# Storing the first six tiles from a second queue and halving the last tile, in an average pool over windows of 16

## The chip, the cores and the metric

The kernel runs on one core of a Trainium2 chip. The core has several engines that run their own instruction streams beside each other. This kernel uses four: VectorE (DVE in the profile), ScalarE (ACT), GpSimd (POOL) and SyncE (SP). Sixteen DMA engines move data between the large memory (HBM) and the core's own memory, which has 128 partitions. DMAs are issued by an engine's instruction stream, and each issuing engine has a DMA queue of its own. The metric is the device time of one launch in microseconds (us); lower is better.

## The reference

The input is float32, 32 x 256 x 4096. Each run of 16 neighbouring values along the last axis is replaced by its mean, so the output is 32 x 256 x 256.

```
for i in range(output_size):
    start = int(i * length / output_size)
    end = int((i + 1) * length / output_size)
    result[:, :, i] = np.mean(x[:, :, start:end], axis=-1)
```

The input has 134.2 MB and the output 8.4 MB.

## The kernel before, in words

Batch and channels are taken together as 8192 rows of 4096 values. The rows are handled in 16 tiles of 512 rows; a tile puts 4 rows on each of the 128 partitions, which is 64 KB per partition and 8.39 MB in all. The first 15 tiles share one layout: each partition owns 60 consecutive rows (`x_many`, `o_many`, lines 46 and 47), and tile t takes 4 of them. The last tile has its own block of 512 rows (`x_last`, `o_last`).

The loop over tiles starts on line 62. A tile is loaded into one of two buffers of `inpool` by one DMA from SP's queue (line 73). The cells (outputs) of a tile, 1024 per partition, are split in two halves of m = 512:

- for the second half, POOL adds the upper 8 values of each window onto the lower 8, in place (line 76);
- for the first half, DVE sums the 16 values of each window (line 81);
- DVE then sums the 8 values that POOL left in each window of the second half (line 84);
- ACT multiplies all 1024 sums by 1/16, in place (line 87).

The results of the first 15 tiles are collected in `res_many` in the core's memory, those of the last tile in `res_last`. Nothing is stored until the last tile's load has been issued. Then one store of `res_many` (7.86 MB, line 75) is issued behind that load on SP's queue. When the last tile is scaled, two more stores from SP write `res_last` (line 93): 120 partitions, then 8.

A load must wait until the buffer that it fills has been read by DVE (line 84, two tiles earlier), and the stores of SP wait for ACT. The waits are set by the framework. The stores are kept out of its bookkeeping of completions and count up a semaphore `stored` instead, on which SP waits at the end (line 98).

Of the kernel before, what the change touches and what calls it, by code (L numbers as in the profile page):

```python
# [1 line left out]

# [4 lines left out]


@with_exitstack
def kernel(  # L10
    ctx: ExitStack,
    tc: tile.TileContext,
    x: bass.AP,
    output_size: int,
    out: bass.AP,
):

    nc = tc.nc
    F32 = mybir.dt.float32
    X = mybir.AxisListType.X

    batch, channels, length = x.shape
    ob, oc, olen = out.shape
    assert ob == batch and oc == channels and olen == output_size
    assert length % output_size == 0
    window = length // output_size  # L30
    hw = window // 2
    inv_w = 1.0 / float(window)

    P = nc.NUM_PARTITIONS
    R = 4
    rows = batch * channels
    assert rows % (P * R) == 0
    ntiles = rows // (P * R)
    many = (ntiles - 1) * R
    cells = R * output_size  # L40
    m = cells // 2
    cols = R * length

    xr = x.rearrange("b c l -> (b c) l")
    orow = out.rearrange("b c o -> (b c) o")
    x_many = xr[0 : P * many, :].rearrange("(p r) l -> p (r l)", p=P, r=many)
    o_many = orow[0 : P * many, :].rearrange("(p r) o -> p (r o)", p=P, r=many)
    x_last = xr[P * many :, :].rearrange("(p r) l -> p (r l)", p=P, r=R)
    o_last = orow[P * many :, :].rearrange("(p r) o -> p (r o)", p=P, r=R)

    res_many = nc.alloc_sbuf_tensor("res_many", [P, (ntiles - 1) * cells], F32, align_bytes=256)
    res_last = nc.alloc_sbuf_tensor("res_last", [P, cells], F32, align_bytes=256)
    inpool = ctx.enter_context(tc.tile_pool(name="inpool", bufs=2))

    stored = nc.alloc_semaphore("stored")

    def store(out, in_):
        ins = nc.sync.dma_start(out=out, in_=in_)
        tc.no_tile_sem_insts.add(ins.ins.name)
        ins.then_inc(stored, 16)  # L60

    for t in range(ntiles):
        last = t == ntiles - 1
        xbuf = inpool.tile([P, cols + 64], F32, name="xin")
        off = 32 if last else 0
        flat = xbuf[:, off : off + cols]
        xin = flat.rearrange("p (o w) -> p o w", w=window)
        if last:
            res, base, src = res_last, 0, x_last
        else:  # L70
            res, base = res_many, t * cells
            src = x_many[:, t * cols : (t + 1) * cols]
        nc.sync.dma_start(out=flat, in_=src)  # L73
        if last:
            store(o_many, res_many[:, :])
        nc.gpsimd.tensor_add(  # L76
            out=xin[:, m:cells, 0:hw],
            in0=xin[:, m:cells, 0:hw],
            in1=xin[:, m:cells, hw:window],
        )  # L80
        nc.vector.reduce_sum(  # L81
            out=res[:, base : base + m], in_=xin[:, 0:m, :], axis=X
        )
        nc.vector.reduce_sum(  # L84
            out=res[:, base + m : base + cells], in_=xin[:, m:cells, 0:hw], axis=X
        )
        nc.scalar.mul(  # L87
            out=res[:, base : base + cells],
            in_=res[:, base : base + cells],
            mul=inv_w,  # L90
        )
    for lo, hi in ((0, 120), (120, P)):
        store(o_last[lo:hi, :], res_last[lo:hi, :])

    ctx.pop_all().close()
    tc.close()
    tc.compile()  # L97
    nc.sync.wait_ge(stored, 48)
    nc.sync.sem_clear(stored)


# [1 line left out]
_INS = ['x', 'output_size']  # L103
_OUTS = [((32, 256, 256), 'float32')]

_NUMBERS = {'output_size': 256}


# [26 lines left out]
```

## Time and profile before

| | us |
|---|---|
| median of 3 runs (lowest to highest) | 333.39 (333.27 to 333.47) |
| span of the profiled execution (its only time in the profile) | 332.2 |
| DVE busy | 209.7 |
| POOL busy | 139.7 |
| ACT busy | 18.2 |
| one load, from one landing to the next | 19.3 |
| DVE's 16-value sums, one (128x512<-128x8192) | 8.69 |
| DVE's 8-value sums, one (128x512<-128x4096) | 4.42 |
| POOL's addition, one | 8.72 |
| ACT's scaling, one | 1.06 |

The span runs from the first to the last instruction of one execution. Busy times of different engines lie beside each other and do not add up to the span. "SPq" in the profile is SP's queue: the times of its rows are those of issuing a DMA, not of the transfer. Rows with "<-" in brackets name what ended the idle time before an instruction.

### The profile page before, as it was taken

How to read it: one execution, taken by the hardware profiler on the slowest of the kernel's cores; microseconds unless marked ns; L12 is line 12 of the kernel's file. 1: busy time of each engine (PE TensorE's matmuls, PEld its weight loads, DVE VectorE, ACT ScalarE, POOL GpSimd, SP SyncE). 2: the span in 40 equal slices, each digit the busy share in tenths (PEclk: the TensorE clock that was granted, in tenths of full speed). 3: DMA queues.
4: the chain of work that ended last, by engine and by line, in shares of the span. 5: the costliest groups of instructions: out<-in, count | busy, mean ns of one | idle time of the engine just before them, and what ended most of it. 6: DMA issues, size and time to landing. Idle time of an engine off the chain costs nothing.

```text
span 332.2 us, 160 instructions
## 1 busy us (share of the span) xinstructions
DVE 209.7 (63%) x32; ACT 18.2 (5%) x17; POOL 139.7 (42%) x20
## 2 busy tenths in 40 slices
DVE  0029396692939669392956939295683929578392
ACT  1000101000010100001010000101000010101001
POOL 0027090642709064370906337090633709063370
DMA  9898989989898999989898998989899998989897
GB/s 379 379 505 379 505 379 442 442 379 505 379 505 379 481 402 402 481 379 505 379 497 387 466 418 379 505 379 505 379 489 395 418 466 379 505 379 505 363 473 300
DMA packets 2599, 142.61 MB, mean 429 GB/s; under 512 B 295, under 2 KB 295, under 8 KB 423
## 3 DMA queue, kind: packets, MB, share of 16 engines
q1 hardware_dynamic: 2599, 142.61, 99.4%
HBM read 134.22 MB, written 8.39 MB: 429 GB/s over the span
## 4 chain that ended last, share of the span: by engine, by line
DMA 66%; POOL 18%; DVE 11%; POOLq 3%; issue 0%; ACT 0%; SPq 0%
DMA xin<-in_x_dram 66%; POOL xin L76 18%; DVE res_many L84 9%; POOLq L97 3%; DVE res_last L84 1%; ACT res_last L87 0%; SPq L73 0%; POOLq L76 0%
## 5 line engine op out<-in xcount | busy, mean ns | idle before, releaser
L76 POOL TENSOR_TENSOR xin<-xin 128x4096 f32<-128x4096 f32 x16 | 139.5, 8719 | 181.9 <-DMA xin<-in_x_dram 181.9
L81 DVE TENSOR_REDUCE res_many<-xin 128x512 f32<-128x8192 f32 x15 | 130.3, 8686 | 107.3 <-DMA xin<-in_x_dram 107.3
L84 DVE TENSOR_REDUCE res_many<-xin 128x512 f32<-128x4096 f32 x15 | 66.3, 4420 | 2.5 <-POOL xin L76 2.3
L87 ACT ACTIVATE res_many<-res_many 128x1024 f32<-128x1024 f32 x15 | 15.8, 1056 | 289.6 <-DVE res_many L84 289.6
L81 DVE TENSOR_REDUCE res_last<-xin 128x512 f32<-128x8192 f32 x1 | 8.7, 8686 | 6.6 <-DMA xin<-in_x_dram 6.6
L84 DVE TENSOR_REDUCE res_last<-xin 128x512 f32<-128x4096 f32 x1 | 4.4, 4420 | 0.2 <-POOL xin L76 0.2
L87 ACT ACTIVATE res_last<-res_last 128x1024 f32<-128x1024 f32 x1 | 1.1, 1056 | 18.8 <-DVE res_last L84 18.8
L87 ACT ACT_TABLE_LOAD x1 | 1.3, 1283 | 0.7 <-PEq L116 0.7
L116 POOL MEMSET const-float32-0.0<- 128x1 f32 x1 | 0.1, 99 | 0.2 <-issue 0.2
L116 POOL MEMSET const-bfloat16-1.0<- 128x1 bf16 x1 | 0.1, 102 | 0.0
L116 POOL MEMSET const-uint8-127<- 128x1 uint8 x1 | 0.1, 102 | 0.0
L116 POOL MEMSET const-float32-1.0<- 128x1 f32 x1 | 0.1, 99 | 0.0
## 6 DMA issues: line engine op xcount, KB each, us to landing
out_dram<-res_many SPq DMA_DIRECT2D x1, 7680.0 KB
out_dram<-res_last SPq DMA_DIRECT2D x1, 480.0 KB
xin<-in_x_dram SPq DMA_DIRECT2D x16, 25.3
out_dram<-res_last SPq DMA_DIRECT2D x1, 32.0 KB
```

Source lines behind the costliest of these rows:

```text
L76: nc.gpsimd.tensor_add(out=xin[:, m:cells, 0:hw], in0=xin[:, m:cells, 0:hw], in1=xin[:, m:cells, hw:window],)
L81: nc.vector.reduce_sum(out=res[:, base : base + m], in_=xin[:, 0:m, :], axis=X)
L84: nc.vector.reduce_sum(out=res[:, base + m : base + cells], in_=xin[:, m:cells, 0:hw], axis=X)
L87: nc.scalar.mul(out=res[:, base : base + cells], in_=res[:, base : base + cells], mul=inv_w,)
L97: tc.compile()
L116: nc = _bacc.Bacc("TRN2", target_bir_lowering=False, num_devices=1)
```

## The change

Three things are done otherwise:

- The results of the first six tiles (`early` = 16 x 3 // 8 = 6, `cut` = 6144 cells per partition, 24 KB of each partition's 60 KB) are stored by a DMA of their own. It is issued by ACT. In the source it stands in the loop behind tile index 7; in the built program it stands on ACT directly behind the scaling of the sixth tile, and waits for that scaling only.
- The store behind the last load, on SP, writes the other nine tiles (4.72 MB).
- The last tile is loaded by two DMAs, each with half of the columns (32 KB per partition, that is two of the four rows), and each half is summed on its own, with POOL, DVE and ACT instructions of half the size. The two stores of the last tile are unchanged.

SP's wait at the end counts four stores instead of three.

```
-    def store(out, in_):
-        ins = nc.sync.dma_start(out=out, in_=in_)
+    def store(out, in_, engine=nc.sync):
+        ins = engine.dma_start(out=out, in_=in_)
         tc.no_tile_sem_insts.add(ins.ins.name)
         ins.then_inc(stored, 16)
+
+    early = ntiles * 3 // 8
+    cut = early * cells
+
+    def sums(xin, res, base, count):
+        h = count // 2
+        nc.gpsimd.tensor_add(
+            out=xin[:, h:count, 0:hw],
+            in0=xin[:, h:count, 0:hw],
+            in1=xin[:, h:count, hw:window],
+        )
+        nc.vector.reduce_sum(out=res[:, base : base + h], in_=xin[:, 0:h, :], axis=X)
+        nc.vector.reduce_sum(
+            out=res[:, base + h : base + count], in_=xin[:, h:count, 0:hw], axis=X
+        )
+        nc.scalar.mul(
+            out=res[:, base : base + count],
+            in_=res[:, base : base + count],
+            mul=inv_w,
+        )
 
     for t in range(ntiles):
...
-        nc.sync.dma_start(out=flat, in_=src)
         if last:
-            store(o_many, res_many[:, :])
...
+            hc = cols // 2
+            for k in range(2):
+                nc.sync.dma_start(
+                    out=flat[:, k * hc : (k + 1) * hc], in_=src[:, k * hc : (k + 1) * hc]
+                )
+            store(o_many[:, cut:], res_many[:, cut:])
+            for k in range(2):
+                sums(xin[:, k * m : (k + 1) * m, :], res, k * m, m)
+        else:
+            nc.sync.dma_start(out=flat, in_=src)
+            sums(xin, res, base, cells)
+        if t == early + 1:
+            store(o_many[:, 0:cut], res_many[:, 0:cut], nc.scalar)
     for lo, hi in ((0, 120), (120, P)):
         store(o_last[lo:hi, :], res_last[lo:hi, :])
...
-    nc.sync.wait_ge(stored, 48)
+    nc.sync.wait_ge(stored, 64)
```

More of the change, by code (lines that the diff above doesn't have):

```diff
@@ L72 @@
             src = x_many[:, t * cols : (t + 1) * cols]
-        nc.sync.dma_start(out=flat, in_=src)
         if last:
-            store(o_many, res_many[:, :])
[L76 to L91, printed above, removed]
+            hc = cols // 2
[11 more added lines that the diff above has]
+            store(o_many[:, 0:cut], res_many[:, 0:cut], nc.scalar)
     for lo, hi in ((0, 120), (120, P)):
```

## The prediction

> **What bounds the kernel now.** I read the busy table and the DMA lines of the page first, then a table of stages, then the waits of the loading queue, then the order in time of the last 27 us.
>
> The page: busy time per engine, packets of the only DMA queue, and the chain that ended last.
>
> ```profile
> span 332.2 us, 160 instructions
> DVE 209.7 (63%) x32; ACT 18.2 (5%) x17; POOL 139.7 (42%) x20
> q1 hardware_dynamic: 2599, 142.61, 99.4%
> HBM read 134.22 MB, written 8.39 MB: 429 GB/s over the span
> DMA 66%; POOL 18%; DVE 11%; POOLq 3%; issue 0%; ACT 0%; SPq 0%
> ```
>
> The chain gives POOL and DVE 29%, but no engine is above 63%, while the packets of the one queue fill 99.4% of the 16 DMA engines' time. The chain goes through POOL and DVE only because a load must wait for a free buffer. Whether that wait ever leaves the DMA engines without work is seen in the stages: one tile period from the start of the run, two from the middle (columns: stretch and its length, busy time of DVE, ACT, POOL, clock, DMA share, GB/s).
>
> ```profile
> 22.50:41.80 19.30, 13.11 (x2) 1.06 (x1) 8.72 (x1) 1.00 1.00 435
> 119.30:138.60 19.30, 13.07 (x3) 1.06 (x1) 8.72 (x1) 1.00 1.00 435
> 138.60:157.90 19.30, 13.04 (x3) 1.06 (x1) 8.72 (x1) 1.00 1.00 435
> ```
>
> Each tile of 8.39 MB takes 19.3 us at a DMA share of 1.00. The arithmetic of a tile (13.1 us of DVE, 8.7 us of POOL beside it) ends 6 us before the next tile lands. The waits of SP's queue and of the engines say the same from the other side:
>
> ```profile
> SPq L73 <- DVE res_many L84: 185.8, 14, 13.3
> SPq L73 <- DMA xin<-in_x_dram: 94.7, 14, 20.9
> DVE res_many L81 <- DMA xin<-in_x_dram: 107.3, 15, 22.5
> ```
>
> A load is issued 13.3 us after the tile before it landed, that is 19.3 - 13.3 = 6.0 us before the DMA engines have finished the load that is running. So the next packets are always queued. Now the end, in order of time:
>
> ```profile
> 301.95 4.42 DVE L84 TENSOR_REDUCE res_many<-xin 128x512 f32<-128x4096 f32 x1 [0.18 <-POOL xin L76]
> 306.40 1.06 ACT L87 ACTIVATE res_many<-res_many 128x1024 f32<-128x1024 f32 x1 [18.25 <-DVE res_many L84]
> 307.48 0.35 SPq L58 DMA_DIRECT2D out_dram<-res_many  x1
> 312.96 8.69 DVE L81 TENSOR_REDUCE res_last<-xin 128x512 f32<-128x8192 f32 x1 [6.59 <-DMA xin<-in_x_dram]
> 313.07 8.72 POOL L76 TENSOR_TENSOR xin<-xin 128x4096 f32<-128x4096 f32 x1 [11.15 <-DMA xin<-in_x_dram]
> 321.82 4.42 DVE L84 TENSOR_REDUCE res_last<-xin 128x512 f32<-128x4096 f32 x1 [0.17 <-POOL xin L76]
> 326.27 1.06 ACT L87 ACTIVATE res_last<-res_last 128x1024 f32<-128x1024 f32 x1 [18.81 <-DVE res_last L84]
> 327.35 0.74 SPq L58 DMA_DIRECT2D out_dram<-res_last  x2
> ```
>
> The big store (15 tiles, 7.86 MB) is queued at 307.48, 5.5 us before the last load lands at 312.96, and runs behind it. The last tile's arithmetic runs beside that store and hands over its 0.5 MB at 327.35.
>
> The trace's packet records price everything the DMA engines do. A 64 KB load packet lasts 2418 ns, a 60 KB packet of the big store 2267 ns, a 4 KB packet of the last store 159 ns, a completion record 9 ns. A load and a store packet cost the same per byte: (2418 - 2267) ns for 4096 bytes is 36.9 ps per byte, 27.1 GB/s per engine. What is left per packet is 2418 - 65536 x 0.0369 = 2 ns, or by the 4 KB packets 159 - 151 = 8 ns. The engine passes from load to store within some 15 ns. One engine's work is 128 load packets (309.5 us, and 0.7 us more because the 16 first packets last 2.9 to 3.4 us), 8 of the big store (18.1) and 8 or so of the last (1.3): 329.6 us. From the first packet's start, 1.0 us after its issue at 0.73, to the last packet's end it is 330.05 us. So no more than 0.5 us of idle time lies inside, and a change can gain only by raising the rate per engine or lose by lowering it, adding packets, or leaving a hole.
>
> **The change, part by part.** The sum is made against the span of 332.2 us; the profiled execution shows no time besides. The median of the runs is 333.39, so 1.2 us lie around the span, and I leave that 1.2 as it is.
>
> Bytes: 142.61 MB before and after. The first six tiles' 3.15 MB only change places: out of the end, into the middle. Per engine that is 8 packets of 24 KB, 8 x 0.91 = 7.3 us. The end gets 7.3 us shorter and the loads get 7.3 us later; sum 0.
>
> Early store: in the built order it stands on ACT behind the sixth scaling, whose end in the trace is 132.51 + 1.06 = 133.57. Issuing takes 0.35 us by SP's row; ACT then idles 18.3 us for the seventh tile, so 0. Behind it on ACT stand the scalings of tiles 7 to 15, for which nobody waits before the late store at the end: were ACT even held until the store landed, 0. It passes nothing on SP or POOL. In the DMA engines it meets the load of tile 7, and the load of tile 8 queued at 132.5. If packets alternate one to one, 8 pairs of 2.42 + 0.91 us make a mixed stage of 26.6 us. Those loads land later, so DVE starts later, but the next load is still queued at least 6 us ahead (its 13.3 us are unchanged and the loads only take longer). No hole.
>
> Extra packets per engine: 8 of the early store (the late one has 8 of 36 KB in place of 8 of 60 KB) and 8 of the halved last load (16 of 32 KB for 8 of 64 KB), 16 at 2 to 8 ns: 0.03 to 0.13 us. Two more completion records, at 9 ns and a gap of some 6: 0.03 us. On the DMA engines, on the path: +0.06 to +0.16; I take +0.1, in the middle.
>
> Mixing loads and stores: not in the trace, where all packets stand in one queue. Lower end: below nothing, if an engine could carry a store beside a load, at most the 7.3 us of the early store hidden. Upper end: each of the 8 store packets sets the engine back as a cold start does (the first packets' +0.7 us): 5.6 us. The nearest row is the change from load to store within the queue at the end, 15 ns at one passage with full rates on both sides, so I take 0.
>
> The Trainium skill speaks to this point, in "DMA: Bandwidth & Descriptors", section "Issuing engines are not separate DMA queues": DMAs of different issuing engines run on the same 16 DMA engines and interleave, and a second issuer saves issue time alone. By it the sum keeps its +0.1, and the lower end of -7.3 falls away. The same page's table under "Latency and other measured facts" has copies between HBM tensors at 214 GB/s per direction as the full rate; taken as 428 GB/s of both together, against the 435 of the stages above, 1.6% of 26.6 us would be an estimated +0.4 us, and the time 333.9. No row of this case shows two queues.
>
> The end: the late store is 8 packets of 36 KB per engine, 8 x 1.36 = 10.9 us, and cover for the last tile is that much in place of 18.1. The halves: the whole load lands at 312.96 + 7.3 + 0.1 = 320.4, the first half 9.65 us earlier, at 310.7. Tile 15 lands 7.4 later too, at 300.4, its DVE work ends at 313.7, its scaling at 314.9, and the late store is issued then, 5.5 us before the last load lands, as before. DVE does the first half from 313.7: 128x256<-128x4096 has as many elements as the 4.42 us row, and 128x256<-128x2048 costs 2.3 by the line through 8192 and 4096 elements (8686 and 4420 ns), ending at 320.4. Second half: POOL 8.72 / 2 = 4.4 from 320.5 beside DVE's 4.42, then 0.2 wait, 2.3 DVE, 0.6 ACT (half of 1.06 and some): issue of the last stores at 327.9, against 327.35. The late store's packets last until 320.4 + 10.9 = 331.3, so 3.4 us are left (3.7 before: 312.96 + 18.1 - 327.35), and after the 1.0 us from issue to first packet 2.4 us. The halving is what keeps it so: a whole last tile would hand over at 320.4 + 14.4 = 334.8. Cost 0, the late store hides it.
>
> Sum: 332.2 + 0.1 = 332.3 span; 333.39 + 0.1 = 333.5 us.
>
> **The rivals.**
> Rival 1, slower: each passage between the queues costs the engine. Place: the mixed stage, 16 passages per engine. For: it is unseen, and the only disturbed packets of the trace, the cold first ones, lost 0.7 us each. Against: the gapless passage at the end. It decides from 0.67 us (0.2%), or 0.57 beyond the 0.1: 36 ns per passage, 2.1% of the stage. At 100 ns it is 1.6 us, 335.1 us; at the upper bound 339.1.
>
> Rival 2, faster: a store reads the chip's memory while a load writes it, and the engine does both at once. For: opposite directions, and the trace never has both. Against: the per-engine rate is the same 27.1 GB/s for both kinds, which looks like one pipe. Full overlap: 333.5 - 7.3 = 326.2 us; a tenth of it is -0.7, 332.8, and that is the point from which it counts. The late store would still cover the end: only the middle shrinks.
>
> Rival 3, slower: the halved tail does not fit under the late store. If a half costs POOL 8.72, DVE 4.42 and ACT 1.06 as the whole does, the last stores are issued at 320.5 + 8.72 + 0.2 + 4.42 + 1.06 = 334.9, the first packet is at 335.9, 8 packets at 0.155 and the landing make a span of 337.7, 338.9 us. Against: DVE's two shapes scale with their elements to 2%.
>
> **How the numbers follow.** About 0.2% (0.67 us) is what a measurement of this kernel can tell from no change. Forecast, DMA time unchanged but for the packets: 0.57, 333.5 us, own range 332.8 to 334.0. Rival 1: 0.28; rival 3: 0.03; together slower 0.31. Rival 2: faster 0.12. The range is 332.7 to 336.0: it leaves out rival 2 (0.12), and above 336.0, where a passage costs more than 150 ns, 0.08.
>
> **What would show it.** In the profile after: a second queue of 3.15 MB; a sum of both queues' packet shares near 99%; a stage from 134 to 160 at 435 GB/s with a share of 1.00; the last load landing near 320.4; the last stores issued near 327.9 and ending 4.4 us later. A mixed stage below 435 GB/s, with longer packets or holes, is rival 1; above 435 GB/s, rival 2; a gap of DMA between late and last store, rival 3. I am wrong if the rate of the mixed stage differs by more than 2%, or if the DMA engines run dry where loads of tiles 7 to 9 meet the store.

## The result

The changed kernel takes 334.15 us (334.02 to 334.43) against 333.39 us (medians of 12 runs each): a ratio of 1.0022, 95% interval 1.0014 to 1.0029. It is slower by 0.76 us, a little more than the 0.67 us that the prediction called the least that can be told from no change, and the interval lies clear of 1. The 333.5 us forecast was too low by 0.65 us; the range 332.7 to 336.0 holds the time. The side on which it fell, slower, had been given 0.31; the case "unchanged but for the packets", with 0.57 and its own range up to 334.0, was missed by 0.15 us.

The span of the profiled execution grew from 332.2 to 332.8 us. What lies around the span is 1.30 us for the changed kernel and 1.31 us for the kernel before, each over the repeated runs, so the whole loss lies inside the span.

The page of the changed kernel: busy times, the two DMA queues, and the chain that ended last.

```profile
span 332.8 us, 166 instructions
DVE 209.6 (63%) x34; ACT 18.4 (6%) x18; POOL 139.9 (42%) x21
q1 hardware_dynamic: 2743, 139.46, 97.2%
q10 hardware_dynamic: 144, 3.15, 2.2%
HBM read 134.22 MB, written 8.39 MB: 429 GB/s over the span
DMA 62%; POOL 21%; DVE 14%; DVEq 1%; issue 0%; ACT 0%; POOLq 0%
```

The same bytes now stand in two queues, and their packets again fill 99.4% of the DMA engines' time (97.2 and 2.2). The DMA engines are the bound as before; DVE and POOL do the same work in the same time. So each engine must have spent more time on the same bytes.

Stages around the early store show where (columns: stretch and its length, busy time of DVE, ACT, POOL, clock, DMA share, GB/s; a packet is counted where it starts, so the cuts lie between packets).

```profile
130.30:135.20 4.90, 2.22 (x1) 1.06 (x1) 0.00 (x0) 1.00 0.99 428
135.20:140.30 5.10, 0.00 (x0) 0.00 (x0) 0.00 (x0) 1.00 0.99 360
140.30:160.23 19.93, 13.10 (x2) 1.06 (x1) 8.72 (x1) 1.00 1.00 434
160.23:179.50 19.27, 13.10 (x2) 0.20 (x1) 8.72 (x1) 1.00 1.00 435
```

The mixed stage proper, 140.30 to 160.23, in which a 64 KB load packet and a 24 KB store packet take turns on every engine, runs at 434 GB/s with the engines full. In the trace's packet records a pair takes 3.32 us there, six times over, where 2418 + 912 ns are 3.33: a passage between the queues costs nothing. The loss lies in the five microseconds before it, at 360 GB/s. There each of the 16 engines has one load packet, started between 135.26 and 135.82, that lasts 2965 to 3494 ns in place of 2418. (The packets last longer while the DMA share is 0.99: the engines are busy, but slower.) It is the packet just ahead of the engine's first store packet. I call the excess the setback: 0.79 us, mean over the engines.

The same thing was in the trace of before, and I had not seen it. The stages around its big store:

```profile
306.60:309.10 2.50, 0.00 (x0) 0.86 (x1) 0.00 (x0) 1.00 0.97 419
309.10:312.00 2.90, 0.00 (x0) 0.00 (x0) 0.00 (x0) 1.00 1.01 362
312.00:330.10 18.10, 13.11 (x2) 1.06 (x1) 8.72 (x1) 1.00 1.00 434
```

The last load packet of each engine, started between 309.12 and 309.66, lasts 2704 to 3159 ns, a setback of 0.50 us, and after it the store runs at full rate. So the change moved a setback that was there and made it larger. Its own late store has none: the packets ahead of it last 1213 ns, all of them.

The end of the changed kernel, in order of time:

```profile
314.53 1.06 ACT L76 ACTIVATE res_many<-res_many 128x1024 f32<-128x1024 f32 x1 [18.30 <-DVE res_many L73]
315.61 0.35 SPq L58 DMA_DIRECT2D out_dram<-res_many  x1
318.74 2.27 DVE L73 TENSOR_REDUCE res_last<-xin 128x256 f32<-128x2048 f32 x1
320.64 4.46 POOL L67 TENSOR_TENSOR xin<-xin 128x2048 f32<-128x2048 f32 x1 [5.18 <-DMA xin<-in_x_dram]
320.94 4.41 DVE L72 TENSOR_REDUCE res_last<-xin 128x256 f32<-128x4096 f32 x1
325.26 2.27 DVE L73 TENSOR_REDUCE res_last<-xin 128x256 f32<-128x2048 f32 x1
327.57 0.63 ACT L76 ACTIVATE res_last<-res_last 128x512 f32<-128x512 f32 x1 [5.89 <-DVE res_last L73]
328.22 0.76 SPq L58 DMA_DIRECT2D out_dram<-res_last  x2
```

The second half lands at 320.6, the last stores are issued at 328.22, and by the packet records the late store's packets end between 330.65 and 331.10, so it hides the hand-over with 2.4 us to spare.

The span's +0.55 us: 0.29 of setback (0.79 - 0.50) and 0.14 of packets (16 of 1213 ns for 8 of 2418 is 0.064; 912 + 1364 for 2267, eight times, is 0.072). The remaining 0.12 is spread over the first packets and the last small stores, and is no more than single executions differ by: the spans of the changed kernel's twelve runs go from 332.7 to 333.1. The medians differ by 0.76 us, 0.2 more than these two executions.

### The profile page after: what moved, and what is told of

Read it like the earlier page. It is cut to its first block, busy times and chain, and to the rows that moved or that the text cites. A ratio compares the mean times of both kernels' runs of the same rounds, so it can differ in the third digit from the quotient of the medians.

```text
span 332.8 us, 166 instructions
## 1 busy us (share of the span) xinstructions
DVE 209.6 (63%) x34; ACT 18.4 (6%) x18; POOL 139.9 (42%) x21
## 3 DMA queue, kind: packets, MB, share of 16 engines
q1 hardware_dynamic: 2743, 139.46, 97.2%
## 4 chain that ended last, share of the span: by engine, by line
DMA 62%; POOL 21%; DVE 14%; DVEq 1%; issue 0%; ACT 0%; POOLq 0%
DMA xin<-in_x_dram 62%; POOL xin L67 21%; DVE res_many L73 11%; DVE res_last L72 3%; DVEq L112 1%; DVE res_last L73 1%; ACT res_last L76 0%; POOLq L67 0%
## 5 line engine op out<-in xcount | busy, mean ns | idle before, releaser
L67 POOL TENSOR_TENSOR xin<-xin 128x4096 f32<-128x4096 f32 (+1 forms) x17 | 139.7, 8216 | 185.0 <-DMA xin<-in_x_dram 185.0
L72 DVE TENSOR_REDUCE res_last<-xin 128x256 f32<-128x4096 f32 x2 | 8.8, 4408 | 0.0
L73 DVE TENSOR_REDUCE res_last<-xin 128x256 f32<-128x2048 f32 x2 | 4.5, 2274 | 0.0
L76 ACT ACTIVATE res_last<-res_last 128x512 f32<-128x512 f32 x2 | 1.3, 630 | 11.4 <-DVE res_last L73 11.4
```

Source lines behind the costliest of these rows:

```text
L67: nc.gpsimd.tensor_add(out=xin[:, h:count, 0:hw], in0=xin[:, h:count, 0:hw], in1=xin[:, h:count, hw:window],)
L72: nc.vector.reduce_sum(out=res[:, base : base + h], in_=xin[:, 0:h, :], axis=X)
L73: nc.vector.reduce_sum(out=res[:, base + h : base + count], in_=xin[:, h:count, 0:hw], axis=X)
L76: nc.scalar.mul(out=res[:, base : base + count], in_=res[:, base : base + count], mul=inv_w,)
```

## The experiments

Where a kernel is a variant of the changed one, its diff is against that, else against the kernel before. Times and ratios are against the kernel before on the same chip. The diffs show the lines that matter, without those between them; left out are `store`'s argument for the engine, where a variant of the kernel before needs it, and the count in SP's wait at the end, which follows the number of stores. Each setback is the mean over the 16 engines in one profiled execution.

**Halving alone, and the early store without a second queue.** Theory A says that the first store of a launch sets the engines back wherever it stands; the rivals blame the second queue (B) or the halving (C).

```
halves_only (against the changed kernel)
-            store(o_many[:, cut:], res_many[:, cut:])
+            store(o_many, res_many[:, :])
-        if t == early + 1:
-            store(o_many[:, 0:cut], res_many[:, 0:cut], nc.scalar)

early_sp (against the changed kernel)
-            store(o_many[:, 0:cut], res_many[:, 0:cut], nc.scalar)
+            store(o_many[:, 0:cut], res_many[:, 0:cut])
```

> The kernel before with the halved last tile alone; one store of 15 tiles from SP. The halved load has 8 more packets per engine, 1213 ns for 32 KB against half of 2418: +0.06 us. Theory A (the setback belongs to the first store of a launch, wherever and from whichever queue): one packet per engine slowed by 0.5 us about 1.6 us after the store's issue, as before; time 333.4 to 333.5. Rival B (the second queue costs the 0.6 us): the same, 333.45. Rival C (the halving costs a good part of it): 333.8 or more.

> The changed kernel with the early store issued from SP, between two loads, no second queue. Theory A: the first store still sets each engine back by 0.5 to 0.8 us, now near 155 us where its turn in SP's queue comes or 1.6 us after its issue at 133.6; the late store sets back nothing; time 333.8 to 334.2. Rival B (the second queue costs the whole 0.6 us): 333.5 us. In between (0.5 us of setback in one queue, 0.8 in another): 333.8.

The halving alone took 333.52 us against 333.46, ratio 1.0003 (0.9994 to 1.0012). The 0.06 us is what its packets were reckoned at, and the upper end of the interval leaves 0.4 us, so C does not explain the loss of 0.76. The setback was 0.15 us in its profiled execution.

The early store from SP took 334.07 us, ratio 1.0019 (1.0010 to 1.0028). That is a loss of 0.61 us with one queue, against 0.76 with two, and the 0.15 between them is less than either interval is wide. B falls as the cause of the whole loss. Here nothing is mixed: in SP's queue the store stands whole between two loads. The stages around it:

```profile
154.60:157.50 2.90, 0.00 (x0) 0.00 (x0) 0.00 (x0) 1.00 1.02 362
157.50:164.90 7.40, 6.45 (x1) 0.00 (x0) 6.34 (x1) 1.00 1.01 434
```

The last load packet ahead of the store is slow again (0.54 us mean), the store itself runs at 434 GB/s. This execution took 333.87 us, 0.20 less than the kernel's median, so its setback may be a small one; whether a second queue adds something to the setback is not settled by these runs. The store was issued at 133.62 and the slow packet started at 154.7, so what goes with the setback is the store's turn on the engine, not its issue. The late store of this kernel had none.

**The big store from ACT, at the end.**

```
act_end (against the kernel before)
-            store(o_many, res_many[:, :])
+            store(o_many, res_many[:, :], nc.scalar)
```

> The kernel before with its one big store issued from ACT in place of SP, at the same place. Bytes and packets as before. Theory A: one setback of 0.5 to 0.8 us about 1.6 us after the issue near 307.5; time 333.4 to 333.7. Rival B (a second queue costs the extra 0.3 us of setback and 0.1 around the span): 333.7 to 333.9. If an idle queue's start is what costs, there are two setbacks, a second one when the last stores go to SP's queue.

334.56 us, ratio 1.0033 (1.0021 to 1.0046), slower than any theory said, for a reason that none of them had. The setback is 0.54 us, as in SP's queue (0.50), and there is no second one. But look at the end:

```profile
307.73 0.37 ACTq L58 DMA_DIRECT2D out_dram<-res_many  x1
315.63 8.69 DVE L81 TENSOR_REDUCE res_last<-xin 128x512 f32<-128x8192 f32 x1 [9.02 <-DMA xin<-in_x_dram]
328.94 1.06 ACT L87 ACTIVATE res_last<-res_last 128x1024 f32<-128x1024 f32 x1 [21.24 <-DVE res_last L84]
330.02 0.77 SPq L58 DMA_DIRECT2D out_dram<-res_last  x2
```

In its own queue the store no longer waits behind the last load but takes turns with it. The last load lands at 315.63 in place of 312.96, the last stores are issued at 330.02 in place of 327.35, only 0.1 to 1.0 us before the big store's packets end, and the end lies open: the big store no longer covers the last stores. Their packets start 0.9 us after the issue and take 0.6 us per engine longer than at 159 ns each. So a second queue does have a price: not in the passages, but in the landing that it puts off.

**The last tile whole.**

```
whole_last (against the kernel before)
-            store(o_many, res_many[:, :])
+            store(o_many[:, 6 * cells :], res_many[:, 6 * cells :])
+        if t == 7:
+            store(o_many[:, 0 : 6 * cells], res_many[:, 0 : 6 * cells], nc.scalar)
```

> The changed kernel without the halving: early store from ACT, last tile loaded and summed whole. The late store (10.9 us) ends near 331.4 and the last tile's hand-over comes 14.4 us after its landing at 320.5, so at 334.9; then 1.0 us to the first packet, 1.4 us of packets and 0.45 us to the span's end: 337.8 us of span, 339.0 us, and 3.5 us or more of idle DMA engines near the end. If the late store hides it in some way I have not seen: 334.1.

340.14 us, ratio 1.0198 (1.0184 to 1.0212).

```profile
320.88 8.69 DVE L81 TENSOR_REDUCE res_last<-xin 128x512 f32<-128x8192 f32 x1 [6.05 <-DMA xin<-in_x_dram]
334.19 1.06 ACT L87 ACTIVATE res_last<-res_last 128x1024 f32<-128x1024 f32 x1 [18.27 <-DVE res_last L84]
335.27 0.74 SPq L58 DMA_DIRECT2D out_dram<-res_last  x2
```

The hand-over is at 335.27, 0.4 later than worked out (the setback moved the landing), and the late store's packets had ended by 331.4. The first small packet starts 0.85 us after its issue, and the small packets take 2.36 us where I had 1.4: 56 of the 128 packets last 171 ns longer than 159 when they run with nothing ahead of them. So without the halving the early store costs 6.6 us; the halving is what the early store needs, as the prediction had it.

**Can a small store take the setback?** If it belongs to the first store as such, a tiny one should take it for the big one.

```
warm_start (against the kernel before)
+    warm = nc.alloc_sbuf_tensor("warm", [P, 128], F32, align_bytes=256)
+    nc.vector.memset(warm[:, :], 0.0)
+    nc.scalar.dma_start(out=o_many[:, 0:128], in_=warm[:, :])

tiny_mid (against the kernel before)
-            store(o_many, res_many[:, :])
+            store(o_many[:, 128:], res_many[:, 128:])
+        if t == 7:
+            store(o_many[:, 0:128], res_many[:, 0:128], nc.scalar)
```

(In the built program the small store of tiny_mid stands behind the first tile's scaling, and is issued at 36.9.)

> The kernel before and one small store more, 512 bytes per partition of zeros from ACT's queue at the very start, overwritten by the big store 300 us later. Theory A: the small store takes the first store's setback, beside the first load's own slow packets; the load packet near 309 us is slowed no more and lasts 2418 ns; time 332.9 to 333.2, faster than before if the two setbacks at the start lie beside each other, 333.4 to 333.5 if they add. Rivals B and C: the packet near 309 us is still slowed by 0.5 us; time 333.4 to 333.6.

> The kernel before with the first 512 bytes per partition of the results stored from ACT's queue after the first tile, near 37 us; the rest at the end from SP as before. Theory A (a price of the first store, not of its bytes): one packet per engine slowed by 0.5 to 0.8 us near 38 us, none near 309; time 333.4 to 333.7. Theory of bytes or of the mixed stage: no setback worth mention near 38 us, 0.5 us near 309 as before; time 333.4. If a queue's start from idle is what costs: both setbacks, 333.9 to 334.2.

warm_start: 333.58 us, ratio 1.0003 (0.9995 to 1.0012); the setback near 309 is still there, 0.40 us. tiny_mid: 333.51 us against 333.51, ratio 1.0000 (0.9991 to 1.0008); no setback near 38 us and next to none (0.03 us) near 309. Theory A as it stood, that the first store pays whatever its size, had the packet near 309 at full speed in both. The two disagree, and so it could be saved only by a cause that tells them apart: the buffer read, or the time. Three kernels were made for that; warm_res and warm_mid are as warm_start, with the zeros read from the results buffer, and with the small store after the first tile.

```
warm_res (against the kernel before)
+    nc.vector.memset(res_many[:, 0:128], 0.0)
+    nc.scalar.dma_start(out=o_many[:, 0:128], in_=res_many[:, 0:128])

warm_mid (against the kernel before)
+    warm = nc.alloc_sbuf_tensor("warm", [P, 128], F32, align_bytes=256)
...
+        if t == 0:
+            nc.scalar.mul(out=warm[:, :], in_=res[:, base : base + 128], mul=0.0)
+            nc.scalar.dma_start(out=o_many[:, 0:128], in_=warm[:, :])

tiny_then_early (against the changed kernel)
+        if t == 1:
+            store(o_many[:, 0:128], res_many[:, 0:128], nc.scalar)
-            store(o_many[:, 0:cut], res_many[:, 0:cut], nc.scalar)
+            store(o_many[:, 128:cut], res_many[:, 128:cut], nc.scalar)
```

> As the kernel before with a small store of zeros at the start, but the zeros come from the place in the results buffer that the first tile fills later. If the setback near 309 us stayed with a store of another buffer because the source had not been read by a DMA yet, it goes now: a packet of 2418 ns near 309, 333.0 to 333.4. If it stayed because the start is too early, or the setback is unsteady from run to run: 0.3 to 0.5 us near 309 again, 333.5.

> The kernel before with a store of 512 bytes per partition of zeros from a buffer of its own after the first tile, near 38 us, to the place that the big store overwrites at the end. If the source matters: 0.4 to 0.5 us of setback near 309 us as in the kernel before, 333.5 to 333.7. If any first store near 38 us takes the setback away: none near 309, 333.4 to 333.5.

> The changed kernel, but the first 512 bytes per partition of the results are stored from ACT after the first tile, and the early store from ACT after the sixth tile takes the rest of the 24 KB. Theory A2 (a setback of the running load at the first store of a launch alone, and a store of 512 bytes takes it nearly free): no packet slowed near 135 us, 0.05 to 0.2 us near 38 us, time 333.5 to 333.7. Rival (a setback whenever a large store begins beside loads on another queue): 0.8 us near 135 us as in the changed kernel, 334.2.

warm_res: 333.67 us, ratio 1.0004 (0.9996 to 1.0013), setback 0.28 us near 309. warm_mid: 333.70 us, ratio 1.0004 (0.9995 to 1.0013), 0.26 us near 309. tiny_then_early: 334.19 us, ratio 1.0021 (1.0012 to 1.0030), 0.87 us near 135. Neither the source nor the time told the two apart: in four of the five kernels a store of 512 bytes per partition did not take the setback away, and theory A in that form falls. tiny_mid's 0.03 us is the odd one out. It is one execution, and I take it for the spread of the setback; that is not shown. That execution has something else of its own: between 130 and 225 us, load packets in some twenty places are up to 0.2 us slow, 0.3 us per engine in all.

**How large must the first store be?** Cut the early store in three; make it smaller; make it one tile.

```
three_act (against the changed kernel)
-        if t == early + 1:
-            store(o_many[:, 0:cut], res_many[:, 0:cut], nc.scalar)
+        if t in (3, 5, 7):
+            lo, hi = (t - 3) * cells, (t - 1) * cells
+            store(o_many[:, lo:hi], res_many[:, lo:hi], nc.scalar)

early_four (against the changed kernel)
-    early = ntiles * 3 // 8
+    early = ntiles // 4

one_tile_early (against the kernel before)
-            store(o_many, res_many[:, :])
+            store(o_many[:, cells:], res_many[:, cells:])
+        if t == 1:
+            store(o_many[:, 0:cells], res_many[:, 0:cells], nc.scalar)
```

> The changed kernel with the early store cut in three of two tiles each, from ACT after tiles 2, 4 and 6. 16 more packets per engine, +0.1 us. Theory A: only the first of the three sets the engines back (0.8 us); time 334.2. If each start of the idle queue costs: three setbacks, +1.6 us, 335.8. If mixing costs by bytes: 334.2 without a setback at one packet.

> The changed kernel with four tiles (16 KB per partition) in the early store in place of six. If the setback of the first store grows with its packet (0.33 us at 8 KB, 0.79 at 24 KB from ACT): 0.5 to 0.6 us at one load packet near 96 us, time 333.9. If its size is chance: anywhere between 0.3 and 0.9. The late store has 44 KB per partition and covers the end more widely.

> The kernel before with the first tile's results (4 KB per partition) stored from ACT after the first tile, the other 14 tiles at the end from SP, the last tile whole. 8 more packets per engine, +0.05 us; the late store's 16.9 us cover the hand-over. If the setback of the first store grows with its packet (0 at 512 bytes, 0.33 us at 8 KB, 0.8 to 1.0 from 16 KB) and a store of a few KB takes it for the later ones: 0.1 to 0.3 us near 38 us, none near 309, time 333.1 to 333.3. If 4 KB is too little to take it: 0.3 to 0.5 us near 309 as well, 333.5 to 333.7. If its size is chance or an early store always costs more: 0.5 us or more near 38, 333.5 to 334.1.

The three early stores of three_act, and the stage of the packet ahead of the first of them:

```profile
L58 ACTq DMA_DIRECT2D out_dram<-res_many x3: 338/338/377, 56.3 to 139.0; - x3
57.90:60.70 2.80, 0.00 (x0) 0.00 (x0) 0.00 (x0) 1.00 0.98 374
```

three_act: 333.69 us, ratio 1.0008 (0.9999 to 1.0017). There is one setback of 0.33 us at the first of the three stores (8 KB packets), none at the second, the third or the late one. That is most of the changed kernel's loss gone, with the same second queue, the same halving and more packets. The theory that each start of an idle queue costs falls.

early_four: 334.27 us, ratio 1.0021 (1.0012 to 1.0029), 0.99 us at 16 KB, where a setback growing evenly with the packet would have had 0.5 to 0.6.

one_tile_early: 334.14 us, ratio 1.0013 (1.0004 to 1.0022), no setback at the 4 KB packets near 38 us and 0.39 us near 310, so 4 KB does not take it either. Its loss lies at the end:

```profile
308.94 0.35 SPq L58 DMA_DIRECT2D out_dram<-res_many  x1
314.24 8.69 DVE L81 TENSOR_REDUCE res_last<-xin 128x512 f32<-128x8192 f32 x1 [6.41 <-DMA xin<-in_x_dram]
328.63 0.76 SPq L58 DMA_DIRECT2D out_dram<-res_last  x2
```

The last stores are issued at 328.63, 1.5 us before the first engine ends its big store, and the last packet ends 2.2 us after the mean end of the big store, in place of 1.4 in the kernel before, where they are issued 2.8 us before that end. My reckoning that 1.0 us from issue to first packet is cover enough was too tight.

All setbacks together, each from one profiled execution ("end open": the end, too, costs time, so the median says nothing of the setback; in the three warm kernels the medians hold 0.22 us per engine of the small store's own packets, 8 of 27 ns):

| first store with packets of 8 KB or more | packet | setback, us | median against before, us |
|---|---|---|---|
| behind the last load, SP: before | 60 KB | 0.50 | - |
| ... warm_start, warm_res, warm_mid | 60 KB | 0.40, 0.28, 0.26 | +0.12, +0.15, +0.18 |
| ... tiny_mid, one_tile_early | 59.5, 56 KB | 0.03, 0.39 | 0.00, (end open) |
| ... halves_only | 60 KB | 0.15 | +0.06 |
| beside the last load, ACT: act_end | 60 KB | 0.54 | (end open) |
| early, ACT: after, whole_last, tiny_then_early | 24 KB | 0.79, 0.85, 0.87 | +0.76, (end open), +0.67 |
| early, ACT: early_four | 16 KB | 0.99 | +0.75 |
| early, SP: early_sp | 24 KB | 0.54 | +0.61 |
| early, ACT: three_act | 8 KB | 0.33 | +0.18 |
| any large store after that, in any kernel | 8 to 44 KB | below 0.05 | - |

In every profiled execution there is one setback per launch, at the first store with packets of 8 KB or more (in tiny_mid it is hardly to be seen), and none at stores of 4 KB or 512 bytes. At the end of the loads it is 0.32 us in the mean of the eight; early, with 16 KB or more, 0.81 us in the mean of five. The difference, 0.49 us, and the 0.14 us of packets make 0.63 us, beside a measured +0.61 to +0.76 us of the kernels with such an early store and a covered end. So the loss is placed: a setback that is larger early than late, and more packets.

What in the chip makes the setback stays open, and so does why it is larger between loads than behind them, and what 8 KB packets do otherwise. The size of the packet was not varied alone, either. The bytes of the store and its place in the launch change with it: the packets of 512 bytes and 4 KB begin at 41 us or before, those of 8 KB at 61, of 16 KB at 100, of 24 KB at 138.6 or later, the largest at about 312. No run here tells the three apart.

## Why the prediction was right or wrong

**The bound** was right: the DMA engines' time decides, and with a covered end it is the sum of their packets, the slow ones counted in.

**Bytes and loads** were right: the end got shorter by what the middle got longer, and no load left a hole. The last load landed at 320.6 (320.4 predicted), the late store was issued at 315.61 (314.9), the last stores at 328.22 (327.9). DVE's halves cost 4.41 and 2.27 us (4.42 and 2.3), POOL's 4.46 (4.4), ACT's 0.63 (0.6).

**Extra packets** were right: 0.14 us, inside 0.06 to 0.16.

**Mixing loads and stores** is the step that failed. I took 0, with ends of -7.3 and +5.6; it is +0.29 us by the two profiled executions, some 0.5 us over all kernels. I took 0 because "the engine passes from load to store within some 15 ns", and that reading was wrong. The gap between the packets is that small, but the load packet ahead of the gap lasts 0.50 us longer, in the very trace I had. I looked at the median duration, 2418 ns, at the gap, and at the slow packets of the start, and not at the 16 slow packets at 309. My own account pointed at them: one engine's work came to 329.6 us of 330.05, and what I left over as at most 0.5 us of idle time is that setback of 0.50. Had I read them, the term would have been "a setback of 0.5 us, moved"; that it grows when it is moved could not have been read there.

**My own sign of being wrong** came true: the stage that I had named from 134 to 160 lost 0.79 us of 26.6, which is 3% and more than the 2% that I allowed. Cut at those times the view even reads as follows, because it counts a packet where it starts:

```profile
133.60:160.20 26.60, 13.10 (x2) 1.06 (x2) 8.72 (x1) 1.00 0.94 394
```

The engines did not run dry there. The loss stands ahead of the first store packet, at 138.6, and the part in which the queues take turns, up to 160.8, has none.

**Rival 1** had the right sign and the wrong place. Passages between the queues cost nothing (3.32 us a pair); the cost is paid once per launch, also without a second queue. Its figures per passage do not apply. That the range holds the time is owed to the room it left for this rival, whose mechanism did not happen: that was luck. **Rival 2** (both directions at once) did not happen: 434 GB/s in the mixed stage, as in a stage of loads. The rule of the Trainium skill, "DMA: Bandwidth & Descriptors", section "Issuing engines are not separate DMA queues", holds here: one queue or two, 334.07 and 334.15 us, losses of 0.61 and 0.76. The 428 GB/s worked out from its table under "Latency and other measured facts" is not what this stage does: it moves 434. **Rival 3** did not happen; whole_last, whose hand-over is as late as that rival's, shows about what it would have cost, 6.6 us.

**What the prediction did not see:** a second queue takes turns with the loads, so at the end it puts off the last landing by 2.7 us (act_end). In the changed kernel the store on ACT was long done by then.

## What to carry to other kernels

Here one resource was full from end to end, and moving its work cost time only in single packets at the seams. In such a case list the slowest packets of each size by the time they start, and don't trust a median and a gap. A store that is moved ahead of its old place takes its cover with it: here the halved last tile was needed to keep the last 0.5 MB hidden, and without it the same early store cost 6.6 us. A store in its own queue shared the engines with the loads beside it, packet by packet, and put off a landing by 2.7 us in act_end, so put it where no landing that matters is near.

## What was not expected of the hardware

- The load packet just ahead of the first large store of a launch lasted 0.03 to 0.99 us longer, in the mean of the engines, than 2418 ns (1213 for the halved load), once per launch; stores of 4 KB and of 512 bytes per packet did not show it, and in five of six kernels did not take it away from the next large one (tiny_mid, with 0.03 us, is the sixth).
- Two queues took turns packet by packet on each engine, 64 KB against 24 KB, at 434 GB/s, with no loss per turn (3.32 us a pair, where the two alone last 3.33).
- In act_end and whole_last, where the end lay open, 4 KB packets of the last stores took up to 288 ns longer than 159 ns, 0.6 us per engine over the last 0.5 MB. In the kernels with a covered end they stayed within 7 ns of it.
